# Sample attention of two head groups: from TensorE products over the cached keys and values to products on ScalarE and VectorE with sums in 32 x 32 squares

## The chip, the cores and the metric

The kernel runs on one core of one Trainium2 chip. That core has TensorE (PE, matrix products, which loads a stationary operand, PEld, and streams a moving one), VectorE (DVE), ScalarE (ACT), GpSimd (POOL) and SyncE (SP, which here does nothing but issue transfers). Every engine works through its own queue in order, and waits on others through semaphores. The scratch memory is SBUF with 128 partitions; products land in PSUM. The metric is the time of one execution on the device in microseconds, lower is better.

## The reference

One layer is computed for a prompt of 256 tokens and for 8 sample sequences of 4 new tokens each (32 sample tokens, 288 tokens in all). A short convolution (mixer A) and a windowed attention (mixer B) work side by side, are gated and added, and a feed-forward block with a convolution follows. All weights are shared by the prompt and the samples.

```
z = x @ w_in                      # h, gate_b, gate_c, q, k, v, g_a, g_b
ya = gate_b * conv3(gate_c * h)
for g, (window, dilation) in enumerate(((128, 1), (512, 4), (2048, 16))):
    # 4 heads of 128; new keys and values are appended to the cache
    idx = l + arange(4)[:, None] - dilation * arange(129)[None, :]
    sc = einsum('nthd,ntjhd->nhtj', q, k_all[:, idx]) * scale - slope * dilation * j
    o, lse = softmax(sc) @ v_all[:, idx], log of its denominator
yb = sum over g of softmax(lse)[g] * o[g]
x1 = LN(ALPHA * x + (sigmoid(g_a) * (ya @ w_a) + sigmoid(g_b) * (yb @ w_b)) @ w_out)
y  = LN(ALPHA * x1 + convffn(x1))
```

What matters here is the sample attention. Group one (dilation 1) has 128 cached keys for each sequence, and its four new tokens share them. In groups two and three (dilations 4 and 16) the four new tokens of a sequence fall on four different residues, so that token t has its own 128 keys: for each sequence, head and t there are 128 keys and 128 values of length 128 which no other token uses. The caches are also outputs, shifted by four rows, so every cached tile is loaded and stored again.

## The kernel before, in words

Tokens are the moving operand of every weight product. Weights come in blocks of 128 output features x 2048 inputs, 1 MB each, loaded by SP (L178, tile `wst`, three buffers). Each block is split in two halves of 1024 columns; for each half ScalarE writes the rounded part (`whi`, L222, the first call of the line) and VectorE the remainder (`wlo`, L222, the second). There are four buffers of halves for each. `product` (L198) takes the block that is ready, calls `prepare` (L173) for the next one, lets the sample attention do one step, and issues 48 matmuls (L216, L217, L218: rounded x rounded, rounded x remainder, remainder x rounded, for 16 slices of 128 inputs) into a PSUM tile `acc` (five buffers).

The products come in this order: 12 for q (numbers 0 to 11, the first three together at L284), 24 for k and v (12 to 35, with the attention of the prompt in between), 48 for mixer A (36 to 83: h, gate_c and gate_b in turn), 32 for the gate of A and w_a in turn (84 to 115), then the gate of B with w_b, which needs the sample attention's result, then w_out and the feed-forward.

The sample attention is a generator, `sample_steps` (L437), advanced once for each product from product 7 on. It passes twice over 18 tiles of 1 MB of cache (keys `ck`, then values `cv`): two tiles of group one (four sequences each), then eight of group two and eight of group three (one sequence each, 128 partitions x 4 heads x 4 t x 128). Tiles of keys have the 128 dimensions on the partitions, tiles of values have the 128 keys there. They go through tag `cache` with three buffers: `fetch` (L418) loads a tile, and its next call stores it to the output.

Every eight products there is a "visit" of three tiles: `by_batch` (L409) writes for each sequence a copy of the queries (or of the softmax weights) in which all columns but the sequence's own are zero (`sw`, L412), and TensorE multiplies it with the tile, head by head, into 32 partitions each (L501). For group one that is a 32 x 128 result; for groups two and three it is 32 x 512, the results of all four tokens with all four token's keys, of which a quarter is wanted. `pick_t` (L430, L433) picks that quarter with four masked multiply-adds on VectorE. The float32 matmuls of L501 show in the trace as two records each. The visits stand in TensorE's queue right between two products (`in_a_row`, `last_mm`).

After the six visits over the keys come the scores of the new keys (L518), `softmax` (L454), `transposed` (L463), six visits over the values with the new values (L509), and at the end a transpose of the result (L536).

`softmax` weights, transposed weights and results lie in `sw2`, the end of the tile `dd`, which mixer A's gated output (`ma`, L642) overwrites column by column.

## Time and profile before

| what | value |
|---|---|
| runs | 1758.19, 1758.09, 1757.65 us, median 1758.09 us |
| span of the profiled execution | 1756.1 us |
| median of the runs beyond that span | 2.0 us |
| PE busy | 1738.7 us, 99% |
| DVE busy | 1009.0 us, 57%, 1320 instructions |
| ACT busy | 797.8 us, 45%, 1142 instructions |
| POOL busy | 244.8 us, 14% |
| cache loads and stores, each | 36 MB in 36 transfers |

The profile gives for the profiled execution no time of its own but its span; what lies around the span is therefore taken as the distance from it to the median of the runs, 2.0 us. Times in the trace are counted from the start of the span. Busy times of PE are those of pipelined matmuls whose recorded spans overlap (a 288-column matmul is recorded with 286 ns, while one starts every 122 ns), so what a stretch of matmuls costs is read from the chain of waits, which goes from end to end.

### The profile page before, as it was taken

What the parts mean: (1) busy time and instruction counts of PE and PEld (TensorE: products, weight loads), DVE (VectorE), ACT (ScalarE), POOL (GpSimd) and SP (SyncE); (2) the same over time, 40 slices, a digit from 0 to 9 for tenths busy, and PEclk for the clock granted to TensorE, in tenths of its full rate; (3) what the DMA queues carried; (4) which work ended last, traced back from release to release, by engine and by line L of the source; (5) the groups of instructions that cost most, each with busy time, mean ns of one, the idle gap of its engine ahead of it and who ended that gap; (6) DMA issues with size and microseconds to landing.
All of it is one profiled execution on the core that took longest, in us unless ns stands there. A gap on an engine that the chain in (4) does not pass through costs nothing.

```text
span 1756.1 us, 33532 instructions
## 1 busy us (share of the span) xinstructions
PE 1738.7 (99%) x14257; PEld 1713.2 (98%) x14257; DVE 1009.0 (57%) x1320; ACT 797.8 (45%) x1142; POOL 244.8 (14%) x404
## 2 busy tenths in 40 slices
PE   9999999999999999999999999999999999999996
PEld 9999999999999999999999999999999999999996
DVE  5444445555555444455588888865555554455554
ACT  5444443343334333344455655544454443344444
POOL 0000000000000000001165323300011110011165
PEclk9999999999999999999999999999999999999998
DMA  9787777877777884467766666565666666666662
GB/s 354 288 331 277 245 280 290 312 298 276 276 287 284 310 311 168 157 245 276 258 240 235 222 223 233 216 238 219 230 226 228 228 223 233 219 237 218 224 219 100
DMA packets 61638, 436.15 MB, mean 248 GB/s; under 512 B 7600, under 2 KB 9648, under 8 KB 17584
## 3 DMA queue, kind: packets, MB, share of 16 engines
q1 hardware_dynamic: 59760, 429.30, 66.2%
q10 hardware_dynamic: 1728, 4.72, 0.7%
q8 instruction: 111, 1.82, 0.4%
q14 instruction: 39, 0.32, 0.1%
HBM read 389.79 MB, written 94.53 MB: 276 GB/s over the span
## 4 chain that ended last, share of the span: by engine, by line
PE 99%; DMA 0%; DVE 0%; ACT 0%; SPq 0%; ACTq 0%; issue 0%; DVEq 0%
PE acc L216 32%; PE acc L218 31%; PE acc L217 31%; PE long L501 1%; PE acc L284 1%; PE att L501 1%; PE att L390 0%; DMA wst<-in_w_in 0%; ACT yah L759 0%; DVE dd L735 0%; PE att L350 0%; PE acc L382 0%; PE att L348 0%; PE att L373 0%; PE att L699 0%; PE att L698 0%
## 5 line engine op out<-in xcount | busy, mean ns | idle before, releaser
L222 DVE TENSOR_TENSOR wlo<-wst,whi 128x1024 fp32r<-128x1024 f32 (+2 forms) x584 | 709.8, 1216 | 600.9 <-ACT whi L222 596.9
L222 ACT CAST whi<-wst 128x1024 fp32r<-128x1024 f32 (+2 forms) x584 | 593.2, 1016 | 888.5 <-PE acc L217 785.0
L216 PE MATMUL acc<-xh,whi 128*128 128x288 f32 (+1 forms) x3216 | 922.4, 287 | 0.0
L217 PE MATMUL acc<-xl,whi 128*128 128x288 f32 (+1 forms) x3216 | 919.5, 286 | 0.0
L218 PE MATMUL acc<-xh,wlo 128*128 128x288 f32 (+1 forms) x3216 | 916.9, 285 | 0.0
L216 PEld LDWEIGHTS acc<-xh,whi 128*128 128x128 f32 x3216 | 605.2, 188 | 6.1 <-issue 6.1
L217 PEld LDWEIGHTS acc<-xl,whi 128*128 128x128 f32 x3216 | 606.4, 189 | 0.0
L218 PEld LDWEIGHTS acc<-xh,wlo 128*128 128x128 f32 x3216 | 605.4, 188 | 0.0
L216 PE MATMUL acc<-yah,whi 128*128 128x288 f32 x1216 | 347.9, 286 | 0.0
L217 PE MATMUL acc<-yal,whi 128*128 128x288 f32 x1216 | 347.7, 286 | 0.0
L218 PE MATMUL acc<-yah,wlo 128*128 128x288 f32 x1216 | 347.7, 286 | 0.0
L216 PEld LDWEIGHTS acc<-yah,whi 128*128 128x128 f32 x1216 | 229.7, 189 | 2.5 <-issue 2.5
L218 PEld LDWEIGHTS acc<-yah,wlo 128*128 128x128 f32 x1216 | 229.8, 189 | 0.0
L217 PEld LDWEIGHTS acc<-yal,whi 128*128 128x128 f32 x1216 | 229.8, 189 | 0.0
L596 POOL COPY qk_s<-u 128x2 f32<-128x2 f32 x44 | 37.9, 862 | 572.6 <-ACT u L810 449.6
L584 DVE SCALAR_TENSOR_TENSOR cy<-u,prm,cy 128x304 f32<-128x304 f32 x120 | 71.0, 592 | 3.8 <-ACT cy L582 0.7
L655 POOL TENSOR_TENSOR ya<-ya,dd 128x288 f32<-128x288 f32 x16 | 13.6, 850 | 304.8 <-DVE ya L654 304.8
L607 DVE TENSOR_TENSOR ya<-cy,acc 128x256 f32<-128x256 f32 x88 | 23.4, 307 | 34.8 <-PE acc L218 34.8
L222 ACT CAST yah<-ya 128x288 fp32r<-128x288 f32 x76 | 32.6, 430 | 16.1 <-POOL ya L655 8.0
L596 POOL COPY cm<-u 128x2 f32<-128x2 f32 x16 | 3.0, 184 | 252.9 <-DVE u L623 252.9
L689 POOL TENSOR_TENSOR cache<-cache,dd 128x288 f32<-128x288 f32 x29 | 29.1, 1003 | 52.5 <-DVE dd L775 33.5
L222 DVE TENSOR_TENSOR yal<-ya,yah 128x288 fp32r<-128x288 f32 x76 | 34.9, 459 | 1.2 <-ACT yah L222 1.2
(176 smaller groups left out, 835.6 us busy)
## 6 DMA issues: line engine op xcount, KB each, us to landing
wst<-in_w_in SPq DMA_DIRECT2D x113, 1024.0 KB, 5.7
wst<-in_w_up SPq DMA_DIRECT2D x88, 1024.0 KB, 4.8
wst<-in_w_down SPq DMA_DIRECT2D x32, 1024.0 KB, 4.8
cache<-in_ck SPq DMA_DIRECT2D x18, 1024.0 KB, 7.8
out_o_ck<-cache SPq DMA_DIRECT2D x18, 1024.0 KB, 7.3
cache<-in_cv SPq DMA_DIRECT2D x18, 1024.0 KB, 6.6
out_o_cv<-cache SPq DMA_DIRECT2D x18, 1024.0 KB, 8.8
wst<-in_w_a SPq DMA_DIRECT2D x16, 1024.0 KB, 5.7
```

The source lines that it names most:

```text
L216: pe.matmul(out, hi[:, c, :], xh_k, start=k == 0, stop=False)
L217: pe.matmul(out, hi[:, c, :], xl_k, start=False, stop=False)
L218: last_mm[0] = pe.matmul(out, lo[:, c, :], xh_k, start=False, stop=k == nk - 1)
L222: return act.copy(hi, src), dve.tensor_tensor(lo, src, f32(hi), ALU.subtract)
L284: i = pe.matmul(o[b], first_w(term == 2, b, k), xk, start=k == 0 and term == 0, stop=k == KD - 1 and term == 2)
L501: row.append(pe.matmul(p[g][j * NS : (j + 1) * NS], sw_m[:, len(row) // NH, j], c[:, o + j * cols : o + (j + 1) * cols], start=b == 0 and ...
L584: dve.scalar_tensor_tensor(y, u[:, i : i + YW], prm[:, w0 + i : w0 + i + 1], y, ALU.mult, ALU.add)
L596: pool.tensor_copy(dst[:, 0:2], u[:, SEQ : SEQ + 2])
L607: dve.tensor_tensor(a, b, c, ALU.mult)
L655: pool.tensor_tensor(m, m, ma[:, i], ALU.add)
L689: pool.tensor_tensor(self.s1, self.s1, d, ALU.add)
```

## The change

Group one, the new keys and values, the softmax and the transposes stay as they are. For groups two and three TensorE no longer multiplies the tiles:

- `weighted` multiplies a tile in place, after it has been stored, two of its four heads at a time (a half). For the even head ScalarE does four multiplications of 128 x 128 by a column of the weights (one for each t); for the odd head VectorE does one of 128 x 512 with the weights broadcast along the last axis. A `tensor_reduce` on VectorE with `apply_transpose=True` then reads the half (1024 columns) in squares of 32 partitions x 32 columns and adds over the 32 partitions of each square: 32 numbers on each partition, written to `parts`.
- In `scores` TensorE adds the four partial sums (one from each block of 32 partitions) by eight matmuls with `parts` as the stationary operand and `squares` (a 0/1 pattern with 32 columns) as the moving one; in `output` eight matmuls with `squares` stationary and `parts` moving add them onto the transposed result of group one, which is now formed by a matmul with the identity instead of a transpose.
- `pick_t`, its mask, the PSUM tile `long` in the sample attention, and the masked copies for groups two and three are gone; `parts` lies in the memory of `sw`.
- The visits are replaced by a list of events, each with the product number from which it is due: a load five products ahead of a tile's place, its store three ahead, the two halves at the place and half a distance later. Tiles of keys of groups two and three stand 2.75 products apart from product 15 on, tiles of values 2.5 apart from product 66 on. The sums of the keys are due at product 59, the softmax at 60, the transposes at 62, the output at 106. The steps begin two products earlier, at product 5.

```diff
+SQ = 32
+SCORES_AT = 13
+TILE_K = 2.75
+VALUES_AT = 64
+TILE_V = 2.5
...
-    sw_m = sb(wk, [P, 2 * NH + 1, NH, NS], "sw", bufs=1)
+    sw = sb(wk, [P, 2 * NT * P + P], "sw", bufs=1)
+    sw_m = sw[:, : 2 * NH * P].rearrange("p (n j r) -> p n j r", n=NB, j=NH)
+    parts = sw[:, : 2 * NT * P].rearrange("p (g k j r) -> p g k j r", g=NG - 1, k=NT, j=NH)
+    squares = sb(big, [P, SQ], "squares")
...
+    def weighted(which, n, half, w):
+
+        c, (g, b) = cache_tiles[which, n], divmod(n - 2, NB)
+        cols = NT * P
+        for j in (2 * half, 2 * half + 1):
+            e = c[:, j * cols : (j + 1) * cols]
+            if j % 2 == 0:
+                for t in range(NT):
+                    e_t = e[:, t * P : (t + 1) * P]
+                    act.activation(e_t, e_t, AF.Copy, scale=w[:, g + 1, j, b * NT + t : b * NT + t + 1])
+            else:
+                e3 = e.rearrange("p (t k) -> p t k", t=NT)
+                w3 = w[:, g + 1, j, b * NT : (b + 1) * NT].unsqueeze(2).broadcast_to([P, NT, P])
+                dve.tensor_tensor(e3, e3, w3, ALU.mult)
+        j = slice(2 * half, 2 * half + 2)
+        dve.tensor_reduce(
+            parts[:, g, :, j, b * NT : (b + 1) * NT].rearrange("p k j t -> p j t k"),
+            c[:, 2 * half * cols : (2 * half + 2) * cols].rearrange("p (j t k c) -> p j t k c", j=2, t=NT, c=SQ),
+            AX.X, ALU.add, apply_transpose=True,
+        )
...
+        def masks(n, w):
+            if n == 0 and w is q_s:
+                dve.reduce_sum(squares, ident.rearrange("p (k c) -> p c k", c=SQ), AX.X)
+            for b in range(4 * n, 4 * n + 4):
+                by_batch(b, w[:, 0], b)
...
+            for g in range(NG - 1):
+                for k in range(NT):
+                    at = g * P + k * SQ
+                    row.append(pe.matmul(
+                        pg[:, at : at + SQ], parts[:, g, k].rearrange("p j r -> p (j r)"), squares, start=True, stop=True
+                    ))
+            in_a_row(row)
+            dve.tensor_tensor(s[:, NG * P :], pn, sbias[:, NG * P :], ALU.add)
+            dve.tensor_tensor(s[:, P : NG * P], pg, sbias[:, P : NG * P], ALU.add)
...
+        def output():
+            po = att(P)
+            row = [last_mm[0], pe.matmul(po, o_sb, ident, start=True, stop=False)]
+            for g in range(NG - 1):
+                for k in range(NT):
+                    row.append(pe.matmul(
+                        po[k * SQ : (k + 1) * SQ], squares, parts[:, g, k].rearrange("p j r -> p (j r)"),
+                        start=False, stop=g == NG - 2,
+                    ))
+            in_a_row(row)
...
+        yield SCORES_AT + 2 + 16 * TILE_K, scores
+        yield SCORES_AT + 3 + 16 * TILE_K, softmax
+        yield VALUES_AT - 2, transposed
+        yield VALUES_AT + 2 + 16 * TILE_V, output
+        for which, w, first, apart in (("ck", q_s, SCORES_AT, TILE_K), ("cv", sT_w, VALUES_AT, TILE_V)):
+            for n in range(N_CT):
+                at = first + n if n < 2 else first + 2 + (n - 2) * apart
+                yield at - 5, partial(cache_load, which, n)
+                yield at - 3, partial(cache_store, which, n)
+                if n < 2:
+                    yield at - 1, partial(masks, n, w)
+                    yield at, partial(first_group, which, n)
+                else:
+                    for half in range(2):
+                        yield at + half * apart / 2, partial(weighted, which, n, half, w)
+
+    events = sorted(sample_events(), key=lambda e: e[0])
```

More of the change, by code (lines that the diff above doesn't have):

```diff
@@ L2 @@
 from contextlib import ExitStack
+from functools import partial
 import numpy as np
@@ L74 @@
 N_WARM = 18
-N_VISIT = 3
-APART = 8
+SQ = 32
[3 more added lines that the diff above has]
+TILE_V = 2.5
 NORM_DVE = ("m", 0, 3), ("r", 0, 3), ("m", 3, 3), ("r", 3, 3), ("m", 6, 2), ("r", 6, 2), ("r", 8, 2), ("r", 10, 2)
@@ L130, in layer_kernel @@
     steps_on = [False]
+    n_product = [2]
     rest = [0]
@@ L202, in product @@
             prepare()
+        n_product[0] += 1
         if steps_on[0]:
@@ L290, in first_three @@
         return [t.rearrange("p a h -> p h a") for t in o]
-    cst = sb(big, [P, C_BM + MASK + NT], "cst")
+    cst = sb(big, [P, C_BM + MASK], "cst")
     pa = sb(big, [P, KD * T], "yal")
@@ L401, in layer_kernel @@
     bmask = cst[:, C_BM : C_BM + MASK]
-    tmask = cst[:, C_BM + MASK :]
-    sw_m = sb(wk, [P, 2 * NH + 1, NH, NS], "sw", bufs=1)
+    sw = sb(wk, [P, 2 * NT * P + P], "sw", bufs=1)
+    sw_m = sw[:, : 2 * NH * P].rearrange("p (n j r) -> p n j r", n=NB, j=NH)
+    parts = sw[:, : 2 * NT * P].rearrange("p (g k j r) -> p g k j r", g=NG - 1, k=NT, j=NH)
+    squares = sb(big, [P, SQ], "squares")
     dd_all = sb(big, [P, KD * T], "dd")
@@ L412, in by_batch, with cache_load, cache_store, sample_events @@
         dve.tensor_tensor(sw_m[:, n], src, m.unsqueeze(1).broadcast_to([P, NH, NS]), ALU.mult)
-    cache_left = iter([(which, n) for which in ("ck", "cv") for n in range(N_CT)])
-    cache_tiles = []
-    to_store = []
-    def fetch():
-        if to_store:
-            sp.dma_start(*to_store.pop())
-        elif len(cache_tiles) < N_VISIT:
-            which, n = next(cache_left, (None, 0))
-            if which:
-                t = sb(wk, [P, 2048], "cache", bufs=3)
-                behind(sp.dma_start(t, ins[which][n]), w_load[0])
-                to_store.append((outs["o_" + which][n], t))
-                cache_tiles.append(t)
-    def pick_t(out, p, add):
-        for t in range(NT):
-            dve.scalar_tensor_tensor(
-                out, p[:, t * P : (t + 1) * P], tmask[:, t : t + 1], add if t == 0 else out, ALU.mult, ALU.add
-            )
-    def sample_steps():
+    cache_tiles = {}
+    def cache_load(which, n):
+        t = sb(wk, [P, 2048], "cache", bufs=3)
+        behind(sp.dma_start(t, ins[which][n]), w_load[0])
+        cache_tiles[which, n] = t
+    def cache_store(which, n):
+        sp.dma_start(outs["o_" + which][n], cache_tiles[which, n])
+    def weighted(which, n, half, w):
[17 more added lines that the diff above has]
+        )
+    def sample_events():
         s = sw2[:, :SW]
@@ L440, in sample_steps @@
         sT = sw2[:, : NG * P].rearrange("p (g r) -> p g r", g=NG)
+        sT_w = sT.rearrange("p g (j r) -> p g j r", j=NH)
         sTn = sw2[: NG * NS, NG * P : NG * P + P]
@@ L443, in sample_steps @@
         o_sb = sw2[:, NG * P + P + NH * P : NG * P + 2 * P + NH * P]
-        held = [(0, range(4)), (0, range(4, NB))] + [(g, (b,)) for g in range(1, NG) for b in range(NB)]
-        def scored(g, p):
-            sg = s[:, g * P : (g + 1) * P]
-            if g == 0:
-                dve.tensor_tensor(sg, p, sbias[:, :P], ALU.add)
-            else:
-                pick_t(sg, p, sbias[:, g * P : (g + 1) * P])
+        p0 = [None]
+        def masks(n, w):
[3 more added lines that the diff above has]
+                by_batch(b, w[:, 0], b)
@@ new lines, in first_group @@
+        def first_group(which, n):
+            if n == 0:
+                p0[0] = att(P)
+            c = cache_tiles[which, n]
+            row = [last_mm[0]]
+            for b in range(4):
+                for j in range(NH):
+                    row.append(pe.matmul(
+                        p0[0][j * NS : (j + 1) * NS], sw_m[:, 4 * n + b, j], c[:, (b * NH + j) * P : (b * NH + j + 1) * P],
+                        start=n == 0 and b == 0, stop=which == "ck" and n == 1 and b == 3,
+                    ))
+            if which == "cv" and n == 1:
+                row += [
+                    pe.matmul(
+                        p0[0][j * NS : (j + 1) * NS], sTn[:, j * NS : (j + 1) * NS], vn[:, j, :], start=False, stop=True
+                    )
+                    for j in range(NH)
+                ]
+            in_a_row(row)
+            if n == 1 and which == "ck":
+                dve.tensor_tensor(s[:, :P], p0[0], sbias[:, :P], ALU.add)
+            elif n == 1:
+                act.copy(o_sb, p0[0])
@@ new lines, in scores @@
+        def scores():
+            pn, pg = att(NG * NS), att((NG - 1) * P)
+            row = [last_mm[0]] + [
+                pe.matmul(
+                    pn[j * NS : (j + 1) * NS, k * NS : (k + 1) * NS], q_s[:, k, j, :], k_s[:, k, j, :],
+                    start=True, stop=True,
+                )
+                for k in range(NG) for j in range(NH)
+            ]
+            for g in range(NG - 1):
[7 more added lines that the diff above has]
+            dve.tensor_tensor(s[:, P : NG * P], pg, sbias[:, P : NG * P], ALU.add)
@@ L454, in softmax @@
         def softmax():
-            dve.tensor_tensor(s[:, NG * P :], pn, sbias[:, NG * P :], ALU.add)
             st = sb(wk, [P, 4], "st", bufs=4)
@@ L464, in transposed @@
             pt, pt2 = att(), att()
-            row = [pe.transpose(pt[:, g * P : (g + 1) * P], s[:, g * P : (g + 1) * P], ident) for g in range(NG)]
+            row = [last_mm[0]]
+            row += [pe.transpose(pt[:, g * P : (g + 1) * P], s[:, g * P : (g + 1) * P], ident) for g in range(NG)]
             row.append(pe.transpose(pt2[: NG * NS, :P], s[:, NG * P :], ident))
@@ L473, in transposed @@
             act.copy(vn, pv[: NG * NS].rearrange("p (j d) -> p j d", j=NH))
-        for values in range(2):
-            p = [None] * NG
-            for first in range(0, N_CT, N_VISIT):
-                here = held[first : first + N_VISIT]
-                for n in range(APART):
-                    fetch()
-                    if values and first == 0 and n == 3:
-                        transposed()
-                    if n == APART - 2:
-                        at = 0
-                        for g, batches in here:
-                            for b in batches:
-                                by_batch(at, sT[:, g].rearrange("p (j r) -> p j r", j=NH) if values else q_s[:, g], b)
-                                at += 1
-                    yield
-                row = []
-                for g, batches in here:
-                    c = cache_tiles.pop(0)
-                    cols = P if g == 0 else NT * P
-                    for b in batches:
-                        if b == 0:
-                            p[g] = p[1] if values and g == 2 else att(P) if g == 0 else (
-                                att() if g == 2 else sb(ps, [P, cols], "long", bufs=1))
-                        o = (b % 4) * NH * P if g == 0 else 0
-                        for j in range(NH):
-                            row.append(pe.matmul(
-                                p[g][j * NS : (j + 1) * NS], sw_m[:, len(row) // NH, j], c[:, o + j * cols : o + (j + 1) * cols],
-                                start=b == 0 and not (values and g == 2), stop=b == NB - 1 and not (values and g < 2),
-                            ))
-                rest_of = [g for g, batches in here if NB - 1 in batches]
-                if values and 0 in rest_of:
-                    row += [
-                        pe.matmul(
-                            p[0][j * NS : (j + 1) * NS], sTn[:, j * NS : (j + 1) * NS], vn[:, j, :], start=False, stop=True
-                        )
-                        for j in range(NH)
-                    ]
-                elif not values and NG - 1 in rest_of:
-                    pn = att(NG * NS)
-                    row += [
-                        pe.matmul(
-                            pn[j * NS : (j + 1) * NS, k * NS : (k + 1) * NS], q_s[:, k, j, :], k_s[:, k, j, :],
-                            start=True, stop=True,
-                        )
-                        for k in range(NG) for j in range(NH)
-                    ]
-                in_a_row(row)
-                for g in rest_of:
-                    if not values:
-                        scored(g, p[g])
-                    elif g == 0:
-                        act.copy(o_sb, p[0])
-                    elif g == NG - 1:
-                        pick_t(o_sb, p[g], o_sb)
-            if not values:
-                softmax()
@@ L534, in sample_steps @@
-        yield
-        po = att(P)
-        pe.transpose(po, o_sb, ident)
-        oT = sw_m[:, 0].rearrange("p j r -> p (j r)")
-        act.copy(oT, po)
-        split(*(h3(t)[:, :, :, P:] for t in (ybh, ybl)), oT.rearrange("p (j a h) -> p j h a", j=NH, h=2))
-        yield
+        def output():
[3 more added lines that the diff above has]
+                for k in range(NT):
+                    row.append(pe.matmul(
+                        po[k * SQ : (k + 1) * SQ], squares, parts[:, g, k].rearrange("p j r -> p (j r)"),
+                        start=False, stop=g == NG - 2,
+                    ))
+            in_a_row(row)
+            oT = sw[:, 2 * NT * P :]
+            act.copy(oT, po)
+            split(*(h3(t)[:, :, :, P:] for t in (ybh, ybl)), oT.rearrange("p (j a h) -> p j h a", j=NH, h=2))
@@ L542, in layer_kernel, with sample_steps @@
+    events = sorted(sample_events(), key=lambda e: e[0])
+    def sample_steps():
+        while events:
+            while events and events[0][0] <= n_product[0]:
+                events.pop(0)[1]()
+            yield
     steps = sample_steps()
@@ L553, in layer_kernel @@
                     (cst[:, :C_BM], ins["cst"][:, :C_BM]),
-                    (cst[:, C_BM : C_BM + MASK], ins["cst"][:, C_MASK : C_MASK + MASK]),
-                    (cst[:, C_BM + MASK :], ins["cst"][:, C_TM:C_M0]),
+                    (bmask, ins["cst"][:, C_MASK : C_MASK + MASK]),
                 ):
                     behind(sp.dma_start(dst, src), w_load[0])
-            steps_on[0] = j * NG + g >= NH * NG - 2 - APART // 2
+            steps_on[0] = j * NG + g >= 4
         pool.tensor_copy(q_s[:, :, j, :].rearrange("p g (a h) -> p g h a", h=2), h3(q_all[:, j])[:, :, :, P:])
@@ L642, in layer_kernel @@
         dve.tensor_tensor(h2(ma[:, i]), h2(sg), o, ALU.mult)
+    n_product[0] += 1000
     for _ in steps:
```

## The prediction

> **What bounds the kernel now.** I read the page first: busy times and the slices.

> ```profile
> span 1756.1 us, 33532 instructions
> PE 1738.7 (99%) x14257; PEld 1713.2 (98%) x14257; DVE 1009.0 (57%) x1320; ACT 797.8 (45%) x1142; POOL 244.8 (14%) x404
> DVE  5444445555555444455588888865555554455554
> PEclk9999999999999999999999999999999999999998
> ```

> TensorE never pauses and runs at its full granted clock; VectorE and ScalarE are about half idle where the sample attention runs (slices 3 to 16). So the kernel is as long as TensorE's queue. The next view, the chain that ended last in order of time (start, length, what), gives what each piece of that queue costs from end to end.

> ```profile
> 95.97 1.89 PE att L501 x64
> 97.85 0.86 PE long L501 x8
> 98.71 0.32 PE acc L216
> ...
> 144.17 0.12 PE acc L216
> 151.17 2.71 PE long L501 x24
> 153.88 0.32 PE acc L216
> ...
> 264.85 1.78 PE att L390 x16
> ...
> 369.46 0.19 PE att L518 x24
> ...
> 668.26 2.71 PE long L501 x24
> ```

> A weight matmul takes 0.12 us. A visit of three tiles of groups two and three takes 2.71 us, and the matmul behind it 0.32 instead of 0.12. There are ten such visits, the first at 151, the last at 668 us (one split between two PSUM tiles), and two mixed ones like that at 96 us. The matmuls by shape confirm the count: 256 records of 512 columns.

> ```profile
> L501 PE MATMUL long<-cache,sw 128*32 128x512 f32 x192 | 22.6, 596 | 0.0
> L501 PE MATMUL att<-cache,sw 128*32 128x512 f32 x64 | 7.5, 595 | 0.0
> ```

> Third, how far ahead of TensorE the weights are prepared: the waits, and a timeline of ScalarE and VectorE.

> ```profile
> ACT whi L222 <- PE acc L217: 274.0, 138, 4.7
> SPq L178 <- DVE wlo L222: 395.0, 85, 7.3
> SPq L426 <- PE long L501: 30.3, 13, 5.5
> ```
> ```profile
> 532.89 1.05 ACT L222 CAST whi<-wst 128x1024 fp32r<-128x1024 f32 x1 [1.91 <-PE acc L217]
> 533.97 1.23 DVE L222 TENSOR_TENSOR wlo<-wst,whi 128x1024 fp32r<-128x1024 f32 x1 [0.48 <-ACT whi L222]
> 538.78 1.05 ACT L222 CAST whi<-wst 128x1024 fp32r<-128x1024 f32 x1 [1.91 <-PE acc L217]
> ```

> ScalarE waits for TensorE to release a half block, not the reverse. The same half of the next product comes at 538.78, so a product takes 5.89 us. With four buffers of halves, a half released in the middle of one product is wanted 1.5 products, 8.8 us, later; its cast and remainder end 2.3 us after the release (532.89 to 535.20). So 6.5 us of delay in these two queues costs TensorE nothing.

> **The change, part by part.** The sum is made against the span of 1756.1 us; the runs' median of 1758.09 lies 2.0 above it, which is added at the end.

> Removed from TensorE: ten visits of 2.71 + 0.32 − 0.12 = 2.91 us, 29.1 us, and 0.86 us in each of the two mixed ones, 1.7 us. Together 30.8 us.

> Added there. (a) Each pass now visits the two tiles of group one separately. At 0.86 us for 8 records, 24 should take 2.58; the visit's 2.71 has 0.13 for coming in, and 0.20 for going out. Two extra visits: 0.7 us. (b) The sums of the keys: eight float32 matmuls, 16 records, with 128 x 128 stationary and 32 columns moving. The nearest row is L390, also 128 x 128 stationary but 128 moving: 1.78 us for 16. No row has this shape with 32 columns; between 0.47 us (16 at the 1.89/64 = 0.030 us of narrow stationary operands) and 3.0 us (16 whole loads of 188 ns, next fence), I take 1.78, since L390's stationary operand is the same. They and the new keys' 24 records (0.19 us, there before) stand in a visit of their own, 0.33 more: 2.1 us. (c) At the end, 16 records with 32 stationary columns, like the 64 at 96 us: 0.030 each, 0.5 us (bound: L390's 0.11 each, 1.8 us), one record more for the identity, 0.1, and a visit's in and out, 0.3: 0.9 us. Added in all 3.7 us (2.3 to 6.2).

> ```profile
> L216 PEld LDWEIGHTS acc<-xh,whi 128*128 128x128 f32 x3216 | 605.2, 188 | 6.1 <-issue 6.1
> ```

> TensorE's balance is −27.1 us (−28.5 to −24.6).

> Now the work that moves to VectorE and ScalarE, from the groups by shape:

> ```profile
> L222 DVE TENSOR_TENSOR wlo<-wst,whi 128x1024 fp32r<-128x1024 f32 x184 | 225.3, 1224 | 244.0 <-ACT whi L222 242.3 <-PE att L501 1.7
> L412 DVE TENSOR_TENSOR sw<-dd,cst 128x128 f32<-128x128 f32 x24 | 6.0, 286 | 6.0 <-PE long L501 5.8
> L364 DVE TENSOR_REDUCE st<-yal 128x1 f32<-128x512 f32 x8 | 5.1, 675 | 0.0
> L433 DVE SCALAR_TENSOR_TENSOR dd<-long,cst,dd 128x128 f32<-128x128 f32 x7 | 2.4, 347 | 0.7 <-PE long L501 0.6
> L222 ACT CAST ybh<-sw 128x128 fp32r<-128x128 f32 x1 | 0.3, 313 | 0.0
> L582 ACT ACTIVATE cy<-u,prm 128x304 f32<-128x304 f32 x16 | 8.7, 544 | 0.0
> L655 POOL TENSOR_TENSOR ya<-ya,dd 128x288 f32<-128x288 f32 x16 | 13.6, 850 | 304.8 <-DVE ya L654 304.8
> ```

> VectorE's two-operand instruction costs (1224 − 286)/896 = 1.05 ns a column and 152 ns fixed: 0.69 us for the 512 columns of a half. The reduce reads 1024 columns; from 675 ns for 512 at 1.05 ns more a column, 1.21 us. That it also crosses 32 partitions is shown nowhere in the trace. Bounds: 0.68 us (the 512-column row itself) and 3.0 us (POOL's 850 ns for 288 columns, the slowest simple row, scaled to 1024). I take 1.21, the same operation's row. [...]

> ScalarE's multiplication of 128 columns by a column of scales: from the cast's 313 ns (no such operand) to L582's 544 (one, but 304 columns); less 176 columns at 0.82 ns (the cast's 1046 ns for 1024 against 313), L582 gives 0.40 us, which I take. [...]

> So a half costs VectorE 0.69 + 1.21 = 1.90 us and ScalarE 1.60. Sixty-four halves: 122 us on VectorE, less 32 masked copies at 0.29 (9 us) and 12 picks at 0.35 (4 us); 102 us on ScalarE. All of it is put beside TensorE's products: a tile of keys gets 2.75 x 5.89 = 16.2 us, one of values 14.7, in which VectorE works 3.8 us (23 and 26%) and ScalarE 3.2 (20 and 22%). The stretches, with PE, PEld, DVE, ACT, POOL busy, granted clock, DMA share and GB/s:

> ```profile
> 95.00:265.00 170.00, 170.00 (x1435) 164.23 (x1435) 79.62 (x123) 72.61 (x111) 6.01 (x12) 1.00 0.75 285
> 245.00:560.00 315.00, 315.00 (x2649) 303.38 (x2648) 172.50 (x263) 128.17 (x166) 9.17 (x65) 1.00 0.77 286
> 560.00:740.00 180.00, 180.00 (x1471) 173.46 (x1470) 80.88 (x85) 65.91 (x75) 0.00 (x0) 1.00 0.64 236
> 875.00:970.00 95.00, 95.00 (x777) 95.00 (x776) 80.00 (x84) 49.43 (x73) 50.53 (x44) 1.00 0.63 235
> ```

> VectorE is now at 47% in the k and v products, 55% in mixer A (some 52 without what is removed), 45% with w_a. It goes to 70, 75 to 78 and 71%; ScalarE to about 62%. At 875 us VectorE is at 84% and TensorE still at 95.00 of 95.00 us. So I price this work at nothing. Without that cover its whole price is the 109 us that VectorE gains.

> The new waits: a reduce waits for ScalarE's four pieces, with VectorE's next remainders (L222) queued behind it; the pieces wait for the tile's store, with ScalarE's next casts behind them; the load of a tile waits for the reduce of the tile three before, where it waited for L501 until now, with weight loads behind it in SP's queue. The delay of the first two is at most 1.60 + 1.90 = 3.5 us, inside the 6.5. For the third, weight loads already stand up to 7.3 us for their own buffers without loss.

> ```profile
> cache<-in_ck SPq DMA_DIRECT2D x15, 1024.0 KB, 6.8
> out_o_cv<-cache SPq DMA_DIRECT2D x18, 1024.0 KB, 8.8
> 420.00:555.00 135.00, 135.00 (x1110) 130.14 (x1103) 70.50 (x100) 52.81 (x65) 3.89 (x28) 1.00 0.82 306
> ```

> Load and store stand two products, 11.8 us, apart, and the store three, 17.7 us, ahead of the first multiplication; they land in 6.8 and 8.8 us. Traffic becomes 1.05 MB for 5.89 us and 2.1 MB for 16.2 or 14.7 us, 307 to 321 GB/s, in an even flow; 306 is carried now without a wait.

> The sum: 1756.1 − 27.1 = 1729.0 us of span, plus 2.0: 1731 us.

> **The rivals.** (1) The joins. TensorE stands at product 59 and 106 until the last reduce is done. That half is due one product earlier, 5.89 us, and needs 3.5 us behind up to 2.45 us of remainders, 5.95 us: the cover is just used up. If it slips by 3 us each time, 6 us are lost: 1737. For it speaks the tight sum; against it, that ScalarE and VectorE are idle a fifth of the time and more, so the half may well begin earlier.

> (2) Queues in the wrong order in mixer A, where VectorE is fullest: 32 halves lie there. If a remainder comes 7 us late instead of 3.5, TensorE stands 0.5 us for each: 16 us, 1747. Against it speaks the stretch at 875 us.

> (3) Slower: crossing the partitions takes several passes, and VectorE becomes the bound. What it has free per tile is 8.6 us (eight tiles beside k and v), 7.8 (eight of keys in mixer A), 7.1 (eight of values there) and 8.1 (eight beside w_a), 252.8 us in all; it needs 1.38 us and two reduces of R for each of 32 tiles. The loss is 64 R + 44.2 − 252.8 us. It begins near R = 2.9 and eats the gain at R = 3.68 us, three times the plain reduce; at four passes, R = 4.84, it is 101 us: 1832 us. For it: no row excludes it. Against it: the row of the plain reduce has no sign of slow reading, and even the slowest row (3.0 us) stays below the point.

> (4) No change: SP stands behind a late reduce so long that weights arrive late, and stalls of 0.42 us a half give the 27 us back: 1758. Its cover is 6.5 us and the third buffer of `wst`; I see nothing that uses it up.

> **How the numbers follow.** Forecast 0.70, at 1731 (1729.6 to 1733.5 by TensorE's own bounds, to 1735 with small waits); joins 0.08; queues 0.09; slower by rival 3 0.11; no change 0.02. The range goes from 1727, a little below TensorE's lower bound because the strips may overlap better, to 1746, which takes in the joins and most of the queues; about a fifth remains outside. A change of 0.2%, 3.5 us, is about what a measurement of this kernel can tell from none: faster 0.70 + 0.08 + 0.09 = 0.87, same 0.02, slower 0.11.

> **What would show it.** Right: TensorE still at 99%, the span near 1729, no 512-column matmuls, L216 to L218 with unchanged durations, a reduce near 1.2 us, a piece on ScalarE near 0.40, VectorE near 1118 us busy, ScalarE near 900. Wrong: waits of TensorE for `wlo` or `whi` (rival 2), for `parts` (rival 1), a reduce above 2.9 us and VectorE at 95% and more (rival 3), or TensorE waiting for `wst` (rival 4).

## The result, and the profile after

| | median us | lowest to highest |
|---|---|---|
| before | 1758.14 | 1757.65 to 1758.23 |
| changed | 1747.74 | 1746.45 to 1749.79 |

The ratio is 0.9943 (95% interval 0.9929 to 0.9957): faster by 10.4 us, 0.6%, where 27 us were forecast. The median lies 1.7 us above the range. The profiled execution has a span of 1744.7 us, 15.7 us above the forecast span of 1729.0.

The page of the changed kernel, the same lines as before:

```profile
span 1744.7 us, 33546 instructions
PE 1717.8 (98%) x14034; PEld 1710.6 (98%) x14034; DVE 1102.0 (63%) x1406; ACT 866.2 (50%) x1398; POOL 260.9 (15%) x404
```

TensorE has lost its 256 wide records, but it is no longer busy without a break. Its waits, taken at the weight loads (PEld), whose times are measured where the ends of matmuls are modelled:

```profile
PEld acc L224 <- DVE wlo L228: 7.4, 11, 1.4
PEld att L356 <- ACT dd L593: 2.8, 1, 2.8
PEld acc L222 <- ACT whi L228: 1.4, 2, 1.2
PEld acc L388 <- DVE yal L374: 0.9, 2, 0.6
```

That is 12.5 us of waiting for halves of weights (L222 and L224 are the old L216 and L218, L228 the old L222), and for prompt attention's operands (L356, L388). A second, smaller part shows in a table by stretches (the columns are those of the prediction's stretches; the third number from the end is the granted clock):

```profile
202.20:205.50 3.30, 3.30 (x15) 3.12 (x14) 3.30 (x4) 3.30 (x8) 0.31 (x1) 0.50 0.89 305
206.00:209.30 3.30, 3.30 (x30) 3.30 (x29) 3.30 (x9) 1.05 (x1) 0.00 (x0) 1.00 0.95 323
625.50:628.70 3.20, 3.20 (x15) 3.20 (x15) 2.96 (x3) 1.01 (x2) 0.00 (x0) 0.50 0.75 279
```

After two of the pauses TensorE ran for 3.4 us at half its clock, 15 matmuls where 30 go at full clock. Each costs 1.7 us. The pauses and the two slow stretches make 12.5 + 3.4 = 15.9 us, which accounts for the 15.7 us that are missing.

What delayed the weights stands in the waits of all engines:

```profile
ACT cache L441 <- DMA out_o_cv<-cache: 71.3, 15, 7.9
ACT cache L441 <- DMA out_o_ck<-cache: 70.4, 16, 9.2
DVE cache L445 <- DMA out_o_ck<-cache: 67.6, 15, 8.4
DVE cache L445 <- DMA out_o_cv<-cache: 54.2, 14, 6.0
```

ScalarE stood 142 us and VectorE 122 us in front of the multiplications (L441, L445), waiting for the tile's store to land. A timeline of ScalarE shows what stands behind (start, length, count, idle before):

```profile
449.42 1.05 ACT L228 CAST whi<-wst 128x1024 fp32r<-128x1024 f32 x1 [1.56 <-PE acc L223]
455.45 2.45 ACT L441 ACTIVATE cache<-cache,dd 128x128 f32<-128x128 f32 x8 [4.99 <-DMA out_o_cv<-cache]
457.80 0.42 ACT L228 CAST yah<-ya 128x288 fp32r<-128x288 f32 x1
458.12 1.99 ACT L228 CAST whi<-wst 128x1024 fp32r<-128x1024 f32 x2
```
```profile
446.01 0.34 SPq L430 DMA_DIRECT2D out_o_cv<-cache  x1
```

The store was issued at 446.01 (SP's own queue) and the multiplication started at 455.45, as soon as it had landed. All eight pieces come at once, though the two halves are due 1.25 products apart, and two casts, 2.0 us, follow that had been ready for 6.0 and 4.0 us (their weights were there and TensorE had released the buffer). Over the 32 tiles of the changed kernel the first half starts 6.1 us (median) after its store is issued and 0.1 us after the store has landed:

```profile
out_o_cv<-cache SPq DMA_DIRECT2D x18, 1024.0 KB, 6.7
```

So the due numbers did not decide. Set against the product that TensorE is at, the first half starts 4.4 products (median) ahead of its due number, and its store 2.5 ahead. The due numbers say only where an instruction stands in the program text; the order of each engine's queue is laid down when the kernel is built, by a planner that moves instructions ahead. ScalarE's queue in the changed kernel shows it at another tile, one of keys (line, output, columns, count):

```
L593 dd     288
L228 whi   1024
L228 whi   1024
L593 dd     288
L385 yal    384
L385 yal    384
L392 yah    512
L392 yah    512
L441 cache  128  x8
L228 whi   1024
L228 whi   1024
```

Both halves (x8) of this tile, due at products 31.5 and 32.875, stand behind the copies of products 24 and 25 (L593, one for each product) and ahead of that of 26. How the planner decides is in no trace; that it goes by durations of its own and takes the transfers for shorter than they are is inferred from this order.

### The profile page after: what moved, and what is told of

Its sections match the earlier page's. It is cut to its first block, busy times and chain, and to the rows that moved or that the text cites. A ratio compares the mean times of both kernels' runs of the same rounds, so it can differ in the third digit from the quotient of the medians.

```text
span 1744.7 us, 33546 instructions
## 1 busy us (share of the span) xinstructions
PE 1717.8 (98%) x14034; PEld 1710.6 (98%) x14034; DVE 1102.0 (63%) x1406; ACT 866.2 (50%) x1398; POOL 260.9 (15%) x404
## 4 chain that ended last, share of the span: by engine, by line
PE 78%; DMA 14%; DVE 3%; issue 2%; ACT 2%; SPq 0%; ACTq 0%; DVEq 0%; POOL 0%; POOLq 0%
PE acc L222 26%; PE acc L224 26%; PE acc L223 26%; DMA cache<-in_cv 4%; DMA cache<-in_ck 4%; DMA out_o_ck<-cache 4%; DMA out_o_cv<-cache 2%; DVE wlo L228 2%; ACT cache L441 1%; PE acc L290 1%; DVE sw L447 1%; DMA dd<-in_w_in 0%; SPq L183 0%; ACT whi L228 0%; ACT yah L789 0%
## 5 line engine op out<-in xcount | busy, mean ns | idle before, releaser
L228 DVE TENSOR_TENSOR wlo<-wst,whi 128x1024 fp32r<-128x1024 f32 (+2 forms) x584 | 704.0, 1211 | 415.3 <-ACT whi L228 413.5
L222 PE MATMUL acc<-xh,whi 128*128 128x288 f32 (+1 forms) x3216 | 922.1, 287 | 0.0
L224 PE MATMUL acc<-xh,wlo 128*128 128x288 f32 (+1 forms) x3216 | 917.9, 285 | 3.1 <-DVE wlo L228 3.0
L228 ACT CAST whi<-wst 128x1024 fp32r<-128x1024 f32 (+2 forms) x584 | 588.8, 1015 | 642.4 <-PE acc L223 591.8
L224 PEld LDWEIGHTS acc<-xh,wlo 128*128 128x128 f32 x3216 | 605.4, 188 | 4.9 <-DVE wlo L228 4.8
L222 PEld LDWEIGHTS acc<-xh,whi 128*128 128x128 f32 x3216 | 605.6, 188 | 1.0 <-issue 0.8
L224 PE MATMUL acc<-yah,wlo 128*128 128x288 f32 x1216 | 348.8, 287 | 1.9 <-DVE wlo L228 1.9
L222 PE MATMUL acc<-yah,whi 128*128 128x288 f32 x1216 | 348.4, 287 | 1.0 <-ACT whi L228 1.0
L224 PEld LDWEIGHTS acc<-yah,wlo 128*128 128x128 f32 x1216 | 230.5, 190 | 2.6 <-DVE wlo L228 2.6
L222 PEld LDWEIGHTS acc<-yah,whi 128*128 128x128 f32 x1216 | 230.4, 190 | 1.2 <-ACT whi L228 1.2
L447 DVE TRANSPOSE_TENSOR_REDUCE sw<-cache 128x32 f32<-128x1024 f32 x64 | 77.2, 1235 | 0.2
L441 ACT ACTIVATE cache<-cache,dd 128x128 f32<-128x128 f32 x128 | 39.6, 389 | 71.3 <-DMA out_o_cv<-cache 71.3
L441 ACT ACTIVATE cache<-cache,qk_s 128x128 f32<-128x128 f32 x128 | 39.7, 389 | 70.4 <-DMA out_o_ck<-cache 70.4
L445 DVE TENSOR_TENSOR cache<-cache,qk_s 128x512 f32<-128x512 f32 x32 | 20.8, 688 | 67.6 <-DMA out_o_ck<-cache 67.6
L685 POOL TENSOR_TENSOR ya<-ya,dd 128x288 f32<-128x288 f32 x16 | 13.6, 851 | 303.6 <-DVE ya L684 303.6
L445 DVE TENSOR_TENSOR cache<-cache,dd 128x512 f32<-128x512 f32 x32 | 20.8, 688 | 54.2 <-DMA out_o_cv<-cache 54.2
## 6 DMA issues: line engine op xcount, KB each, us to landing
wst<-in_w_in SPq DMA_DIRECT2D x113, 1024.0 KB, 6.8
wst<-in_w_up SPq DMA_DIRECT2D x88, 1024.0 KB, 4.8
wst<-in_w_down SPq DMA_DIRECT2D x32, 1024.0 KB, 4.8
cache<-in_ck SPq DMA_DIRECT2D x18, 1024.0 KB, 8.0
out_o_ck<-cache SPq DMA_DIRECT2D x18, 1024.0 KB, 6.5
cache<-in_cv SPq DMA_DIRECT2D x18, 1024.0 KB, 8.3
out_o_cv<-cache SPq DMA_DIRECT2D x18, 1024.0 KB, 6.7
wst<-in_w_a SPq DMA_DIRECT2D x16, 1024.0 KB, 5.1
```

The source lines that it names most:

```text
L222: pe.matmul(out, hi[:, c, :], xh_k, start=k == 0, stop=False)
L224: last_mm[0] = pe.matmul(out, lo[:, c, :], xh_k, start=False, stop=k == nk - 1)
L228: return act.copy(hi, src), dve.tensor_tensor(lo, src, f32(hi), ALU.subtract)
L441: act.activation(e_t, e_t, AF.Copy, scale=w[:, g + 1, j, b * NT + t : b * NT + t + 1])
L445: dve.tensor_tensor(e3, e3, w3, ALU.mult)
L447: dve.tensor_reduce(parts[:, g, :, j, b * NT : (b + 1) * NT].rearrange("p k j t -> p j t k"), c[:, 2 * half * cols : (2 * half + 2) * cols ...
```

## The experiments

Three theories were tried: that the multiplications stand too early in the queues (the queue theory), that VectorE has too much to do, and that loads and stores take longer than their distances allow. All runs were compared with the kernel before.

### Both multiplications held until they are due

```diff
-                    act.activation(e_t, e_t, AF.Copy, scale=...)
+                    behind(act.activation(e_t, e_t, AF.Copy, scale=...), w_split[0])
...
-                dve.tensor_tensor(e3, e3, w3, ALU.mult)
+                behind(dve.tensor_tensor(e3, e3, w3, ALU.mult), w_split[1])
```

`w_split` holds the cast and the remainder of the second half block that was last prepared; `behind` orders the queue without a semaphore.

> ScalarE's pieces are held behind the cast, and VectorE's 128 x 512 product behind the remainder, of the second half block that the same product prepares, so that neither can stand in its queue ahead of its due product. Queue theory (the multiplications stand about three products too early in the in-order queues, wait there for the store to land, and hold up casts and remainders): the waits of L441 and L445 for the stores (70 to 140 us per line now) fall below 10 us in all, TensorE's pauses go, span 1729 to 1731, time 1731 to 1733. Full-engine theory (VectorE has too much to do): the work is the same, so pauses stay, 1744 to 1750. Late-transfer theory (loads and stores take longer than the distances of two and three products allow): waits for the stores stay above 50 us, 1744 to 1750.

Measured: 1730.30 us (1729.87 to 1730.84), ratio to before 0.9842 (0.9827 to 0.9856); the span is 1729.0 us (1728.1 to 1729.0 in its four executions), the forecast's own number. The page and the stretches of this run:

```profile
span 1729.0 us, 33546 instructions
PE 1711.6 (99%) x14034; PEld 1707.4 (99%) x14034; DVE 1108.2 (64%) x1406; ACT 872.4 (50%) x1398; POOL 250.5 (14%) x404
```
```profile
400.00:550.00 150.00, 150.00 (x1276) 149.31 (x1275) 109.29 (x147) 82.60 (x146) 8.98 (x30) 1.00 0.84 309
550.00:740.00 190.00, 190.00 (x1562) 189.68 (x1561) 113.45 (x116) 91.22 (x147) 1.59 (x2) 1.00 0.67 241
```

No wait for a store is left, TensorE is busy throughout, and VectorE has slightly more busy time than in the changed kernel. The first half now starts 28.1 us (median) after its store, the second 9.7 us after the first. The casts show the same: worked out from the traces, a cast started up to 9.0 us after its weights were there and its buffer was free in the changed kernel, 15 of them (over products 5 to 102) later than the 6.5 us of cover; here the latest is 1.1 us late. Only the queues' order differs, so the loss was the order.

### Only ScalarE held

The first of the two edits alone.

> Only ScalarE's pieces are held behind the cast; VectorE's product of a half may still stand early and wait for the store. Queue theory: ScalarE's waits for stores go, VectorE's 122 us stay; since remainders follow casts, a part of TensorE's pauses (waits for wlo) stays, 1733 to 1743, between the changed kernel and the one with both held. If casts alone are what is late: 1731. Full-engine and late-transfer theories: 1744 to 1750.

Measured: 1737.71 us (1733.70 to 1738.14), ratio 0.9879 (0.9864 to 0.9893), inside the queue theory's range. Its waits:

```profile
DVE cache L445 <- DMA out_o_ck<-cache: 52.2, 16, 6.5
DVE cache L445 <- DMA out_o_cv<-cache: 50.3, 13, 6.2
```
```profile
PEld acc L224 <- DVE wlo L228: 7.4, 5, 2.6
```

VectorE still stands 102.5 us for stores, and TensorE waits for remainders and, but for 0.2 us, not for casts: 7.4 us, about the 7.3 us by which the span (1736.3) lies over 1729.0.

### Only VectorE held

The second edit alone.

> The counterpart of the run with ScalarE held: VectorE's 128 x 512 product is held behind the due product's remainder, ScalarE's pieces may stand early and wait for the store. Queue theory: ScalarE's waits for stores stay near 140 us, VectorE's go; casts come late, so pauses on whi and on wlo stay, 1733 to 1745. Full-engine theory: 1744 to 1750 (but the run with both held has spoken against it).

Measured: 1760.14 us (1758.50 to 1762.56), ratio 1.0013 (1.0004 to 1.0023). The queue theory's range was missed by 15 us on the far side: this half of the cure undoes the whole gain. TensorE's waits, and two slow stretches:

```profile
PEld acc L224 <- DVE wlo L228: 11.1, 14, 1.0
PEld acc L222 <- ACT whi L228: 8.3, 9, 1.9
PEld acc L388 <- DVE yal L374: 5.2, 2, 4.4
```
```profile
176.20:181.00 4.80, 4.80 (x22) 4.80 (x21) 2.57 (x3) 0.59 (x1) 0.00 (x0) 0.50 0.92 343
328.20:331.30 3.10, 3.10 (x15) 3.10 (x15) 3.10 (x5) 0.19 (x1) 1.05 (x2) 0.50 0.98 312
```

The pauses are twice those of the changed kernel: 24.6 us, with 10.2 us at half clock (5.1 us lost), 29.7 against the 29.3 us that this span (1758.3) lies over 1729.0. And this although ScalarE waits hardly longer for stores than in the changed kernel (145 against 142 us):

```profile
DVE wlo L228 <- ACT whi L228: 211.3, 74, 7.9
...
ACT cache L441 <- DMA out_o_cv<-cache: 77.1, 15, 8.3
ACT cache L441 <- DMA out_o_ck<-cache: 68.2, 15, 8.4
```

VectorE now stands 211 us for casts, up to 7.9 us at a time (88 us over the same stretch of the changed kernel, at most 2.7). The total alone is no sign of harm: with both held it is 172 us, at most 2.9. The reading that a late cast leaves VectorE idle, and that its own half comes afterwards, ahead of the next remainder, is tried in the next run.

### Only VectorE held, and VectorE's halves made small

The edit is against the run before this one. The reduce now reads 32 of VectorE's own columns and none of ScalarE's.

```diff
-                behind(dve.tensor_tensor(e3, e3, w3, ALU.mult), w_split[1])
+                behind(dve.tensor_tensor(e3[:, :, :8], e3[:, :, :8], w3[:, :, :8], ALU.mult), w_split[1])
-        j = slice(2 * half, 2 * half + 2)
+        j = slice(2 * half + 1, 2 * half + 2)
...
-            parts[:, g, :, j, b * NT : (b + 1) * NT].rearrange("p k j t -> p j t k"),
-            c[:, 2 * half * cols : (2 * half + 2) * cols].rearrange(...)
+            parts[:, g, :1, j, b * NT : b * NT + 1].rearrange("p k j t -> p j t k"),
+            c[:, (2 * half + 1) * cols : (2 * half + 1) * cols + SQ].rearrange(...)
```

> As the run with only VectorE held (1760.1 us), but VectorE's product covers 32 columns instead of 512 and its reduce 32 instead of 1024 (most of the sums of groups two and three are left out), so its 1.9 us a half become about 0.4. Loads, stores and ScalarE's pieces are as there. If the extra loss of that run came from VectorE's halves standing in front of remainders that the waiting casts had already made late: most of the 25 us of pauses go, 1733 to 1745. If ScalarE's waits for the stores alone make the casts too late: 1752 to 1760, with ScalarE's waits near 145 us.

Measured: 1752.14 us (1750.58 to 1753.87), ratio 0.9965 (0.9953 to 0.9978), at the lower edge of the second case. VectorE is back at 1010.7 us of busy time, near the 1009.0 before the change, and 21.2 us of the 29.3 remain (span 1750.2). ScalarE's waits are 68.5 and 66.1 us. So ScalarE's early waits alone are enough to make the casts too late (up to 9.4 us here); the other 8 us are gone once VectorE's halves are small. No reduce of the run before waited for ScalarE's pieces, so it is not that wait that was saved. Why holding VectorE costs more than leaving both early (15.7 us) is not settled beyond these 8 us. That the two engines' waits for the same landing overlap when both stand early is a likely part of it, argued and not tried.

### Loads and stores 1.5 products earlier

```diff
-                yield at - 5, partial(cache_load, which, n)
-                yield at - 3, partial(cache_store, which, n)
+                yield at - 6.5, partial(cache_load, which, n)
+                yield at - 4.5, partial(cache_store, which, n)
```

> Loads and stores of the cache are due 1.5 products (8.8 us) earlier, nothing else. Late-transfer theory: the stores land 8.8 us sooner before the multiplications, waits for them fall from 263 us by half or more, 1731 to 1738. Queue theory: the multiplications follow the stores forward in the queues, so the waits stay at 150 to 270 us and the time at 1742 to 1752. Full-engine theory: 1744 to 1750.

Measured: 1752.82 us (1748.84 to 1759.88), ratio 0.9972 (0.9959 to 0.9985). Not faster, rather slower than the changed kernel; the median is just above the queue theory's range.

```profile
ACT cache L441 <- DMA out_o_cv<-cache: 68.9, 14, 7.2
...
ACT cache L441 <- DMA out_o_ck<-cache: 51.7, 14, 6.5
```

The waits on both engines fall only from 263 to 220 us, and the first half still starts 6.5 us (median) after its store: the multiplications moved forward with the stores. The late-transfer theory falls.

### The reduce on half the columns

```diff
-        j = slice(2 * half, 2 * half + 2)
+        j = slice(2 * half, 2 * half + 1)
...
-            c[:, 2 * half * cols : (2 * half + 2) * cols].rearrange(...)
+            c[:, 2 * half * cols : (2 * half + 1) * cols].rearrange(...)
```

> The reduce reads only the even head's 512 columns of each half (the odd heads' sums are left out), so VectorE has 64 x 0.54 = 35 us less to do; transfers and multiplications are as in the changed kernel. Full-engine theory: most of the 12 us of pauses go, 1731 to 1736. Queue theory: the waits for the stores stay near 260 us, 1743 to 1750. Late-transfer theory: the same as the queue theory.

Measured: 1747.72 us (1746.67 to 1749.20), ratio 0.9941 (0.9927 to 0.9956), the changed kernel's time.

```profile
L447 DVE TRANSPOSE_TENSOR_REDUCE sw<-cache 128x16 f32<-128x512 f32 x64 | 44.6, 706 | 6.1 <-ACT cache L441 5.0
```

33 us less work on VectorE (44.6 us here, 77.2 in the changed kernel) brought nothing, and the waits for stores are 280 us, near the 260 that the queue theory expected. So VectorE's fullness was not the cause.

### Held, but up to three products early

The first run's edits, with the half block prepared three products before.

> Both multiplications held as in the run with both held, but behind the half block prepared three products earlier, so they may stand up to three products (17.7 us) ahead of their due number. There, with both held, the first half starts 28.1 us (median) after its store is issued, and stores land in 6 to 7 us; three products less leaves some 10 us. If only the wait for the landing does the harm: few waits (under 40 us in all), 1730 to 1733. If standing ahead of casts and remainders does harm by itself: 1736 to 1745.

Measured: 1730.28 us (1730.16 to 1731.50), ratio 0.9846 (0.9829 to 0.9862), with no wait for a store. Its premise was off: the first half starts 20.4 us (median; least 7.6) after the store, not 10. What it shows is that standing somewhat early does no harm as long as the store has landed; it doesn't reach the point where harm begins.

### Held, with the tiles two products apart

```diff
-TILE_K = 2.75
+TILE_K = 2.0
...
-TILE_V = 2.5
+TILE_V = 2.0
```

> Both held as in the first run, and the tiles two products apart instead of 2.75 and 2.5, so VectorE works 3.9 us for a tile in 11.8 us, 33% on top of some 52, about 85%, and transfers take 356 GB/s while it lasts. If VectorE has room: 1730 to 1733. If it is near its limit or the transfers are: pauses of TensorE for wlo or whi, 1735 to 1745.

Measured: 1730.26 us (1729.90 to 1731.34), ratio 0.9844 (0.9830 to 0.9859). Where the values are being multiplied:

```profile
400.00:520.00 120.00, 120.00 (x1031) 119.31 (x1031) 91.61 (x126) 68.10 (x126) 8.43 (x26) 1.00 0.89 331
```

VectorE at 76% and the transfers at 0.89 leave TensorE without a pause. The three held versions (1730.26 to 1730.30 us) beat both kernels and cannot be told apart.

## Why the prediction was right or wrong

**TensorE's balance was right.** −27.1 us was forecast, a span of 1729.0 us, and with the order mended the span is 1729.0. That it agrees to 0.1 us is luck, as the four executions of that run span 0.9 us and the terms below are off by about 0.1 us each; that it agrees to 1 us is not. The added pieces, the first two in the changed kernel's chain of waits, the last in that of the run with both held:

```profile
84.03 1.01 PE att L476 x32
85.05 0.32 PE acc L222
...
385.05 1.90 PE att L506 x16
```
```profile
661.18 0.22 PE att L536 x2
661.40 0.57 PE att L539 x16
661.98 0.32 PE acc L222
```

The visit to a tile of group one takes 1.01 + 0.20 us, against 0.95 + 0.13 + 0.20 in the sum. The keys' sums take 1.90 against 1.78; taking the row with the same stationary operand was right, though only 32 columns move. The output takes 0.22 + 0.57 + 0.20, against 0.9.

**The durations were right.** From the groups by shape:

```profile
L447 DVE TRANSPOSE_TENSOR_REDUCE sw<-cache 128x32 f32<-128x1024 f32 x64 | 77.2, 1235 | 0.2
L441 ACT ACTIVATE cache<-cache,qk_s 128x128 f32<-128x128 f32 x128 | 39.7, 389 | 70.4 <-DMA out_o_ck<-cache 70.4
L445 DVE TENSOR_TENSOR cache<-cache,qk_s 128x512 f32<-128x512 f32 x32 | 20.8, 688 | 67.6 <-DMA out_o_ck<-cache 67.6
```

The reduce takes 1.235 us (forecast 1.21), a piece 0.389 (0.40), the product 0.688 (0.69). Crossing 32 partitions costs next to nothing over a plain reduce (706 ns for 512 columns in the run with half the reduce, 675 for the plain one), one column in 1.03 ns (from 512 to 1024 columns); rival 3 falls with it. ScalarE's load was set too high: eight pieces take 2.45 us, so they overlap, 0.31 us each; its busy time grew by 68 us instead of 102, VectorE's by 93 instead of 109.

**The step that failed** is the one on the new waits: "the delay of the first two is at most 1.60 + 1.90 = 3.5 us, inside the 6.5", resting on "the store three, 17.7 us, ahead of the first multiplication". It took the due numbers for the order of the queues. The store's landing stood between store and multiplication as the trace of before had it (8.8 us), but I never asked where in ScalarE's and VectorE's queues the multiplications would come. They came right behind the store, and then the wait in front of them is the landing, up to 9.2 us on ScalarE, and 2.45 us for all eight pieces behind it, not 1.60. Casts came up to 9.0 us late by it, past the 6.5 us of cover. What the prediction priced at nothing cost the span 12.5 us of pauses and 3.4 us at half clock. The waits of before could be read as a hint: SP's loads of `cache` stood up to 5.5 us in its queue for L501, so an instruction can stand microseconds ahead of what it waits for. There it hurt no one, since the visits were tied to TensorE's order and only SP stood waiting. The change moved such a wait onto the two engines that feed TensorE.

**The rivals.** Rival 2 came nearest, and by its mechanism: casts, and with them remainders, come more than 6.5 us late. That its 1747 us meets the measured 1747.74 is luck, as it counted 0.5 us for each of 32 halves and nothing for a slow clock. It was wrong in its place and cause: the pauses lie beside k and v too (199 us), and come from the queue order and the stores, not from VectorE's fullness in mixer A. Its chance, 0.09, was too low because the stretch at 875 us was taken as evidence against it: that stretch shows a full VectorE, not one that stands waiting. Rival 1 didn't happen: TensorE's waits show none at L506 or L539, which read `parts`. Rival 4's queue, SP, was the wrong one of the three.

## What to carry to other kernels

When an engine's queue also feeds the bottleneck, cost a new instruction by the latest thing that it waits for and by where the queue puts it, and not by its duration. A due number in the program text is a wish unless something holds the instruction back: look at the laid-down queue, and where an instruction that waits for a transfer stands ahead of work that is ready, order it behind that work. Here such an ordering edge, without a semaphore, was worth 17 us, and it has to be given to both engines: given to VectorE alone it left the kernel no faster than the one before.

## What was not expected of the hardware

| run | pauses us | at half clock us | sum | span over 1729.0 |
|---|---|---|---|---|
| changed | 12.5 | 6.8 | 15.9 | 15.7 |
| only ScalarE held | 7.6 | 0 | 7.6 | 7.3 |
| only VectorE held | 24.6 | 10.2 | 29.7 | 29.3 |
| only VectorE held, halves small | 17.0 | 6.8 | 20.4 | 21.2 |
| transfers earlier | 14.5 | 10.2 | 19.6 | 20.1 |
| half the reduce | 16.9 | 0 | 16.9 | 17.9 |

The changed kernel's trace shows what came before its two slow stretches (the columns as above; the slow stretches are the second and the fourth line):

```profile
198.73:202.14 3.41, 0.79 (x6) 0.57 (x5) 2.28 (x3) 2.35 (x6) 0.37 (x1) 1.00 0.74 305
202.14:205.55 3.41, 3.41 (x16) 3.23 (x15) 3.41 (x4) 3.41 (x8) 0.37 (x1) 0.50 0.88 305
621.98:625.39 3.41, 1.29 (x9) 0.86 (x8) 3.41 (x4) 3.41 (x6) 0.00 (x0) 1.00 0.00 0
625.40:628.80 3.40, 3.40 (x16) 3.40 (x16) 3.06 (x3) 1.11 (x2) 0.00 (x0) 0.50 0.76 282
```

Both slow stretches are 3.413 us long in the trace's record of the clock. In the 3.41 us just before each, TensorE's weight loads stood idle for 2.84 and 2.55 us in sum. Counted in lengths of 3.413 us from 4.17 us, where the record of the clock begins at full, the slow stretches begin 58.0 and 182.0 lengths later; in no other such length up to the last matmul did the weight loads stand idle for more than 1.52 us. So both falls of the clock in this trace follow idle time that came together within 3.41 us, one pause of 2.8 us or two of 1.2 and 1.4. Where the limit lies, and why the pause of 2.8 us in the run with half the reduce brought no slow stretch, is not shown.
